# Moving three products of the last Strassen block into the accumulation banks of the plain products, and splitting the last one

## The chip, the cores and the metric

The kernel runs on one core of a Trainium2 chip. The metric is the device time of one execution in microseconds. A profiled execution has a span of its own (first to last instruction), which is a little shorter than its device time.

## The reference

One layer of a decoder trunk on x (512 tokens x 1024). The change touches only the second half of the layer: the squared-ReLU MLP, its addition to the residual stream, and the last LayerNorm.

```python
m = mixer(x, w_in[i], ...)                       # three attention branches, gates, output projection
x = layer_norm(DEEPNORM_ALPHA * x + m, ln1_g[i], ln1_b[i])
hid = jax.nn.relu(x @ w_up[i])                   # 512 x 4096
c = jnp.square(hid) @ w_down[i]                  # 512 x 1024
ple = jax.nn.sigmoid(x @ w_ple_gate[i]) * (p[i] @ w_ple[i])
x = layer_norm(DEEPNORM_ALPHA * x + c + ple, ln2_g[i], ln2_b[i])

def layer_norm(x, g, b):
    mu = x.mean(-1, keepdims=True)
    var = jnp.square(x - mu).mean(-1, keepdims=True)
    return (x - mu) * lax.rsqrt(var + LN_EPS) * g + b
```

## The kernel before

**Numbers as pairs.** Each fp32 matrix is held as a high and a low part in the type fp32r (`h`, `l` or `lo`), and each product of two matrices is three matmuls: high by high, high by low, low by high. A matmul has 128 x 128 weights and up to 512 moving columns, and its result fills a PSUM bank of 128 x 512.

**The list of items.** All large products stand in one list, `items`. An item has its matmuls (`mm`), an evacuation (`ev`) that takes the result out of its bank, the weight chunks that it needs (`need`) and those that it sets free (`c`). The loop at L1157 goes through them in order: an item's evacuation is written down before the matmuls of the next. Banks come from `mm_bank` (two, in turn) or `at_bank` (six). Inside each engine the framework's scheduler then decides the order of the instructions, by its own estimates of when their inputs are there; the engine executes that order strictly.

**Weights.** A chunk of weights is loaded by SP's DMA queue into one of four `raw` buffers, cast to its high part by ScalarE (L209) and its low part taken by VectorE (L210). The pairs lie in rings `wh` and `wl` of seven slots each (`RING`); a slot is taken from those that are free, and a cast waits until one is. `pump` allows a chunk's split as soon as fewer than seven chunks before it are unreleased by the list.

**The MLP.** The 32 column tiles of the hidden layer are made by `up(f)`, 24 matmuls of 512 columns each. The down projection consumes four hidden tiles in a block: seven blocks (`nb = 7`) go by a Strassen scheme, with seven half-size products instead of eight, and the last four tiles by ordinary products, `plain`. A Strassen product `down(b, p, r, ...)` with `p` from 1 to 7 and `r` the upper or lower half of its rows has six matmuls. Products 1, 6 and 7 stay in six `at` banks over all blocks and are combined after the last (L643 to L655). Products 2, 3, 4 and 5 get a bank for each block, and their evacuation adds the result (L638) to one of the eight tiles `acc[tt, half]`: the residual stream in row blocks `tt` = 0 to 3 of 128 tokens and two halves of 512 columns. Products 2, 3 and 4 go to (r, 0), (r, 1) and (r + 2, 0).

`plain` goes through the pairs (tt, half) in the order (0,0), (0,1), (1,0), ... (3,1). Each is a group of 12 matmuls (L668 to L670) in a bank from `mm_bank`; L674 adds the bank to `acc[tt, half]`. For half 0 the first and third of the four plain weight chunks are used in turn, for half 1 the second and fourth. When both halves of a row block are there, its LayerNorm and the two DMAs to the output follow. "Rows 2" below means the row block tt = 2.

**Two LayerNorms.** Rows 0 to 2 use `layer_norm_act`: two passes of ScalarE for the row sums (L425), the mean (L427), two passes of ScalarE for the squares (L429), two small operations (L431, L432), a power on GpSimd (L433), and two scalings of each half on VectorE (L435, L437). Rows 3 use `layer_norm`: `bn_stats` over each half (L408), its aggregate (L410), L412, the power on GpSimd (L413), and scalings L415 and L417.

Of the kernel before, what the change touches and what calls it, by code (L numbers as in the profile page):

```python
# [12 lines left out]
AF = mybir.ActivationFunctionType  # L13
OP = mybir.AluOpType
# [3 lines left out]
P = 128  # L18
FF = 4096
ALPHA = 2.0 ** 0.25  # L20
EPS = 1e-5
# [34 lines left out]
def trunk(tc, a, out):  # L56
    nc = tc.nc
    es = ExitStack()
    with es:
# [14 lines left out]
        def slot(name, dt=F32):  # L74
            return big.tile([P, 512], dt, name=nm(name), tag="s", bufs=NSLOT)

        def small(name, n):
            return one.tile([P, n], F32, name=nm(name), tag=f"sm{n}", bufs=12 if n < 8 else 8)
# [64 lines left out]
        loads, sums, chunks, placed = [], [], [], []  # L143
# [21 lines left out]
        def chunk(src, w):  # L165
            return chunk_of(load(src, w))
# [58 lines left out]
        def item(cs, mm, ev, need=None, bank=None):  # L225
            items.append({"c": cs, "mm": mm, "ev": ev, "need": need, "bank": bank})
# [166 lines left out]
        acc = {}  # L393
        lnc = {}
# [22 lines left out]
                nc.vector.scalar_tensor_tensor(ts[h], ts[h], r, lnc[b][h], op0=OP.mult, op1=OP.add)  # L417
                fin(h, ts[h])

        def layer_norm_act(ts, g, b, fin):  # L420

            sm, sq = small("lsm", 2), small("lsq", 2)
            junk = slot("junk")
            for h in range(2):
                nc.scalar.activation(junk, ts[h], AF.Copy, accum_out=sm[:, h:h + 1])  # L425
            nmu = small("lnm", 1)
            nc.vector.tensor_scalar(nmu, sm[:, 0:1], sm[:, 1:2], -1.0 / D, op0=OP.add, op1=OP.mult)  # L427
            for h in range(2):
                nc.scalar.activation(junk, ts[h], AF.Square, bias=nmu, accum_out=sq[:, h:h + 1])  # L429
            r = small("lr", 1)  # L430
            nc.vector.tensor_scalar(r, sq[:, 0:1], sq[:, 1:2], 1.0 / D, op0=OP.add, op1=OP.mult)  # L431
            nc.vector.tensor_scalar(r, r, EPS, None, op0=OP.add)  # L432
            nc.gpsimd.tensor_tensor(r, r, mhalf, OP.pow)  # L433
            for h in range(2):
                nc.vector.scalar_tensor_tensor(ts[h], ts[h], nmu, lnc[g][h], op0=OP.add, op1=OP.mult)  # L435
            for h in range(2):
                nc.vector.scalar_tensor_tensor(ts[h], ts[h], r, lnc[b][h], op0=OP.mult, op1=OP.add)  # L437
                fin(h, ts[h])
# [109 lines left out]
        left = {}  # L548
# [6 lines left out]
        def mlp_items():  # L555
            nb = 7
# [57 lines left out]
            def down(b, p, r, c, free=()):  # L614

                last = b == nb - 1
                stays = p in (1, 6, 7)

                def bank():
                    if b == 0:  # L620
                        keep[p, r] = at_bank()
                    return keep[p, r]

                def mm(ps):
                    q = slice(r * P, r * P + P)
                    for i in range(2):
                        h, lo = left[2 * b + i, p]
                        s = slice(i * 512, i * 512 + 512)
                        go = i == 0 and (b == 0 or not stays)
                        end = i == 1 and (last or not stays)  # L630
                        nc.tensor.matmul(ps, h[:, q], c["h"][:, s], start=go, stop=False, skip_group_check=True)  # L631
                        nc.tensor.matmul(ps, h[:, q], c["l"][:, s], start=False, stop=False, skip_group_check=True)  # L632
                        nc.tensor.matmul(ps, lo[:, q], c["h"][:, s], start=False, stop=end, skip_group_check=True)  # L633

                def ev(ps):
                    if not stays:
                        t = acc[{2: (r, 0), 3: (r, 1), 4: (r + 2, 0), 5: (r + 2, 1)}[p]]
                        nc.vector.tensor_add(t, t, ps)  # L638
                    if (p, r) in ((6, 0), (7, 0)):
                        left_rest()  # L640
                    if not last:
                        return
                    if p == 1:  # L643
                        p1s[r] = slot("p1s")
                        nc.scalar.copy(p1s[r], ps)
                        nc.vector.tensor_add(acc[r, 0], acc[r, 0], ps)
                    elif p == 6:
                        v3[r] = slot("v3")
                        nc.vector.tensor_sub(v3[r], ps, p1s[r])
                        nc.vector.tensor_add(acc[r, 1], acc[r, 1], v3[r])  # L650
                        nc.vector.tensor_add(acc[r, 1], acc[r, 1], acc[r + 2, 1])
                    elif p == 7:
                        nc.vector.tensor_add(v3[r], v3[r], ps)
                        nc.vector.tensor_sub(acc[r + 2, 0], acc[r + 2, 0], v3[r])
                        nc.vector.tensor_add(acc[r + 2, 1], acc[r + 2, 1], v3[r])  # L655
                item(list(free), mm, ev, need=[c], bank=bank if stays else None)

            def plain(cs):

                for tt in range(4):  # L660
                    for half in range(2):
                        def mm(ps, tt=tt, half=half):
                            q = slice(tt * P, tt * P + P)
                            for i in range(4):
                                h, lo = left[4 * nb + i]
                                c = cs[i % 2, half]
                                s = slice((i // 2) * 512, (i // 2) * 512 + 512)
                                nc.tensor.matmul(ps, h[:, q], c["h"][:, s], start=i == 0, stop=False)  # L668
                                nc.tensor.matmul(ps, h[:, q], c["l"][:, s], start=False, stop=False)
                                nc.tensor.matmul(ps, lo[:, q], c["h"][:, s], start=False, stop=i == 3)  # L670

                        def ev(ps, tt=tt, half=half):
                            t = acc[tt, half]
                            nc.vector.tensor_add(t, t, ps)  # L674
                            if half:
                                def fin(h, y):
                                    (nc.sync if h else nc.scalar).dma_start(
                                        out[0, tt * P:tt * P + P, 512 * h:512 * h + 512], y)
                                norm = layer_norm if tt == 3 else layer_norm_act
                                norm([acc[tt, 0], acc[tt, 1]], "ln2_g", "ln2_b", fin)  # L680
                        item(list(cs.values()) if (tt, half) == (3, 1) else [], mm, ev, need=list(cs.values()))

            for f in range(4):
                up(f)
            for b in range(nb):
                wd = a["wd"][b]
                ld = lambda i: load(wd[i].rearrange("p k n -> p (k n)"), 1024)
                up(4 * b + 4)
                s11 = ld(0)
                s12 = ld(1)  # L690
                t1 = total(s11, s12)
                c5 = chunk_of(t1)
                c1 = chunk_of(s11)
                down(b, 5, 0, c5)
                down(b, 1, 0, c1)
                down(b, 5, 1, c5, [c5])
                cu = up(4 * b + 5, False)
                s22 = ld(3)
                t2 = total(t1, s22)
                t3 = total(s12, s22)  # L700
                c3 = chunk_of(s22)
                c6 = chunk_of(t2)
                down(b, 3, 0, c3)
                down(b, 1, 1, c1, [c1, cu])
                down(b, 6, 0, c6)
                down(b, 3, 1, c3, [c3])
                cu = up(4 * b + 6, False)
                s21 = ld(2)
                c2 = chunk_of(s21)
                down(b, 2, 0, c2)  # L710
                down(b, 6, 1, c6, [c6, cu])
                down(b, 2, 1, c2, [c2])
                up(4 * b + 7)
                c7 = chunk_of(t3)
                c4 = chunk_of(total(t2, s21))
                down(b, 4, 0, c4)
                down(b, 7, 0, c7)
                down(b, 7, 1, c7, [c7])
                down(b, 4, 1, c4, [c4])
            wd = a["wd"][nb]  # L720
            plain({(i // 2, i % 2): chunk(wd[i].rearrange("p k n -> p (k n)"), 1024) for i in range(4)})

        wout_at = len(items)
        ple_items()
# [17 lines left out]
        mhalf = one.tile([P, 1], F32, name="mhalf")  # L742
# [79 lines left out]
        for i in range(2):  # L822
            nc.vector.scalar_tensor_tensor(lamt[:, 2 * i, :], lamt[:, 2 * i, :], 1.0, lamt[:, 2 * i + 1, :],
                                           op0=OP.mult, op1=OP.mult, accum_out=lp[:, i:i + 1])
# [332 lines left out]
        for n, it in enumerate(items):  # L1157
# [3 lines left out]
            need = it["need"] or it["c"]  # L1161
# [18 lines left out]
            ps = it["bank"]() if it["bank"] else mm_bank()  # L1180
# [106 lines left out]
```

## Time and profile before

| what | value |
|---|---|
| median of 3 runs | 1104.25 us (1103.94 to 1104.48) |
| profiled execution: device time | 1104.82 us |
| profiled execution: span | 1103.1 us |
| mean granted TensorE clock | 0.996 |
| TensorE matmul busy | 1084.1 us (98%) |
| VectorE busy | 682.4 us (62%) |
| ScalarE busy | 481.7 us (44%) |
| GpSimd busy | 38.8 us (4%) |

How to read the rows: `PE` is TensorE's matmuls, `PEld` its weight loads, `DVE` VectorE, `ACT` ScalarE, `POOL` GpSimd, `SP` SyncE; a name with a q (`ACTq`) is that engine's queue issuing something. A row of a timeline gives start (us), duration (us), engine, line, operation, tiles written and read, shape, and in brackets the idle time of the engine before it with what ended that. A row of a group ends in its busy time, the mean in ns of one and the idle time before them. A row of the windows gives the stretch, its length, the busy time of each engine, the granted clock, the DMA engines' busy share, and GB/s.

### The profile page before, as it was taken

How to read it: one execution, taken by the hardware profiler on the slowest of the kernel's cores; microseconds unless marked ns; L12 is line 12 of the kernel's file. 1: busy time of each engine (PE TensorE's matmuls, PEld its weight loads, DVE VectorE, ACT ScalarE, POOL GpSimd, SP SyncE). 2: the span in 40 equal slices, each digit the busy share in tenths (PEclk: the TensorE clock that was granted, in tenths of full speed). 3: DMA queues.
4: the chain of work that ended last, by engine and by line, in shares of the span. 5: the costliest groups of instructions: out<-in, count | busy, mean ns of one | idle time of the engine just before them, and what ended most of it. 6: DMA issues, size and time to landing. Idle time of an engine off the chain costs nothing.

```text
span 1103.1 us, 13166 instructions
## 1 busy us (share of the span) xinstructions
PE 1084.1 (98%) x5032; PEld 898.6 (81%) x5032; DVE 682.4 (62%) x1216; ACT 481.7 (44%) x803; POOL 38.8 (4%) x74
## 2 busy tenths in 40 slices
PE   8999999999999999899999999999999999999996
PEld 5888788999888887778888888888888888888884
DVE  6868466564253758654444354875676686686676
ACT  7656444343232545453233232333554454454433
POOL 1000200000000000000000020110000000000000
PEclk9999999999999999999999999999999999999999
DMA  8222422131222103113322344243222322322302
GB/s 271 103 96 84 135 77 77 39 102 50 98 77 87 59 27 105 58 52 102 105 86 96 105 143 163 77 153 113 97 96 77 134 96 80 131 96 95 115 1 76
DMA packets 31327, 105.71 MB, mean 96 GB/s; under 512 B 3962, under 2 KB 4106, under 8 KB 31264
## 3 DMA queue, kind: packets, MB, share of 16 engines
q1 hardware_dynamic: 28080, 96.48, 25.6%
q0 software_dynamic: 2608, 7.35, 2.2%
q10 hardware_dynamic: 576, 1.05, 0.3%
q8 instruction: 39, 0.64, 0.2%
q14 instruction: 24, 0.20, 0.1%
HBM read 102.74 MB, written 2.12 MB: 95 GB/s over the span
## 4 chain that ended last, share of the span: by engine, by line
PE 90%; DVE 5%; ACT 2%; issue 1%; DMA 1%; POOL 1%; SPq 0%; DVEq 0%; ACTq 0%; POOLq 0%
PE mm L88 17%; PE mm L89 17%; PE mm L87 17%; PE mm L299 3%; PE mm L301 3%; PE mm L300 3%; PE mm L632 2%; PE mm L631 2%; PE mm L633 2%; PE at L632 2%; PE at L631 2%; PE at L633 2%; PE mm L462 1%; PE mm L460 1%; PE mm L527 1%; PE mm L528 1%
## 5 line engine op out<-in xcount | busy, mean ns | idle before, releaser
L209 ACT CAST wh<-raw 128x1024 fp32r<-128x1024 f32 (+2 forms) x176 | 180.4, 1027 | 295.9 <-PE mm L88 237.9
L210 DVE TENSOR_TENSOR wl<-raw,wh 128x1024 fp32r<-128x1024 f32 (+2 forms) x176 | 209.0, 1192 | 120.8 <-ACT wh L209 119.2
L87 PE MATMUL mm<-xhT,wh 128*128 128x512 f32 x512 | 203.1, 397 | 0.9 <-DVE da_qb L108 0.7
L88 PE MATMUL mm<-xlT,wh 128*128 128x512 f32 x512 | 200.9, 392 | 1.6 <-DVE xlT L210 1.6
L89 PE MATMUL mm<-xhT,wl 128*128 128x512 f32 x512 | 201.2, 393 | 0.5 <-DVE wl L210 0.5
L88 PEld LDWEIGHTS mm<-xlT,wh 128*128 128x128 f32 x512 | 96.5, 188 | 22.4 <-DVE xlT L210 3.5
L87 PEld LDWEIGHTS mm<-xhT,wh 128*128 128x128 f32 x512 | 96.6, 189 | 20.6 <-DVE da_qb L108 1.1
L89 PEld LDWEIGHTS mm<-xhT,wl 128*128 128x128 f32 x512 | 96.3, 188 | 20.5 <-DVE wl L210 1.0
L88 PE MATMUL mm<-x1lT,wh 128*128 128x512 f32 x256 | 99.6, 389 | 0.0
L89 PE MATMUL mm<-x1hT,wl 128*128 128x512 f32 x256 | 99.6, 389 | 0.0
L87 PE MATMUL mm<-x1hT,wh 128*128 128x512 f32 x256 | 99.6, 389 | 0.0
L299 PE MATMUL mm<-wh,xhT 128*128 128x512 f32 x160 | 65.5, 410 | 0.0
L300 PE MATMUL mm<-wl,xhT 128*128 128x512 f32 x160 | 63.2, 395 | 0.0
L301 PE MATMUL mm<-wh,xlT 128*128 128x512 f32 x160 | 63.2, 395 | 0.0
L87 PEld LDWEIGHTS mm<-x1hT,wh 128*128 128x128 f32 x256 | 48.1, 188 | 10.0
L89 PEld LDWEIGHTS mm<-x1hT,wl 128*128 128x128 f32 x256 | 48.1, 188 | 10.0
L88 PEld LDWEIGHTS mm<-x1lT,wh 128*128 128x128 f32 x256 | 48.1, 188 | 9.9
L209 ACT CAST wh<-wsum 128x1024 fp32r<-128x1024 f32 x28 | 29.5, 1053 | 52.7 <-PE mm L88 49.3
L210 DVE TENSOR_TENSOR wl<-wsum,wh 128x1024 fp32r<-128x1024 f32 x28 | 34.3, 1224 | 23.7 <-ACT wh L209 23.1
L638 DVE TENSOR_TENSOR xn<-xn,mm 128x512 f32<-128x512 f32 x56 | 38.2, 682 | 9.9 <-PE mm L633 9.8
L632 PE MATMUL mm<-wl,hh 128*128 128x512 f32 x112 | 43.6, 389 | 0.0
L631 PE MATMUL mm<-wh,hh 128*128 128x512 f32 x112 | 43.6, 389 | 0.0
(302 smaller groups left out, 1948.9 us busy)
## 6 DMA issues: line engine op xcount, KB each, us to landing
raw<-in_wt_dram SPq DMA_DIRECT2D x63, 512.0 KB, 3.3
raw<-in_wu_dram SPq DMA_DIRECT2D x32, 512.0 KB, 3.3
raw<-in_wd_dram SPq DMA_DIRECT2D x32, 512.0 KB, 3.2
raw<-in_wv_dram SPq DMA_DIRECT2D x20, 512.0 KB, 3.3
raw<-in_wb_dram SPq DMA_DIRECT2D x8, 512.0 KB, 3.3
raw<-in_wo_dram SPq DMA_DIRECT2D x8, 512.0 KB, 3.6
raw<-in_wg_dram SPq DMA_DIRECT2D x8, 512.0 KB, 5.0
rawx<-in_xT_dram SPq DMA_DIRECT2D x8, 256.0 KB, 7.2
```

What stands on the lines that cost most here:

```text
L87: nc.tensor.matmul(ps, wh, xh, start=start, stop=False, skip_group_check=True)
L88: nc.tensor.matmul(ps, wh, xl, start=False, stop=False, skip_group_check=True)
L89: nc.tensor.matmul(ps, wl, xh, start=False, stop=stop, skip_group_check=True)
L209: nc.scalar.copy(h, raw)
L210: nc.vector.tensor_sub(lo, raw, h.bitcast(F32))
L299: nc.tensor.matmul(ps, x1, c["h"][:, s], start=k == 0, stop=False)
L300: nc.tensor.matmul(ps, x1, c["l"][:, s], start=False, stop=False)
L301: nc.tensor.matmul(ps, x2, c["h"][:, s], start=False, stop=k == 7)
L631: nc.tensor.matmul(ps, h[:, q], c["h"][:, s], start=go, stop=False, skip_group_check=True)
L632: nc.tensor.matmul(ps, h[:, q], c["l"][:, s], start=False, stop=False, skip_group_check=True)
L633: nc.tensor.matmul(ps, lo[:, q], c["h"][:, s], start=False, stop=end, skip_group_check=True)
L638: nc.vector.tensor_add(t, t, ps)
```

## The change

In the last Strassen block (b = 6) the products 2, 3 and 4, six items of six matmuls, are no longer items. Their matmuls open the bank of the plain group that adds to the same tile, so six of the eight groups have more matmuls: (0,0), (1,0) take product 2, (0,1), (1,1) product 3, and (2,0), (3,0) product 4. The weight chunks `c2`, `c3` and `c4` and the hidden tiles of these products are held until the lower half has read them: until (1,0), (1,1) and (3,0). Number and size of the chunks' loads and rings stay.

For rows 0 to 2 the addition becomes a `scalar_tensor_tensor` with an accumulator output, which writes the row sum of its half; the two ScalarE passes of `layer_norm_act` for the sums are gone.

For rows 3 the banks come from `at_bank`; the group (3,1) is cut into two parts of 256 columns with a bank each. Every part's addition is followed by `bn_stats` over it, and a new `last_norm` aggregates three sets of statistics, scales the two halves by L415's operation, and then makes L417's operation in three parts (512, 256 and 256 columns), each with its own output DMA on the SP, ScalarE and SP queues.

```diff
-        def layer_norm_act(ts, g, b, fin):
+        def layer_norm_act(ts, sm, g, b, fin):
 
-            sm, sq = small("lsm", 2), small("lsq", 2)
+            sq = small("lsq", 2)
             junk = slot("junk")
-            for h in range(2):
-                nc.scalar.activation(junk, ts[h], AF.Copy, accum_out=sm[:, h:h + 1])
...
-            def plain(cs):
+            def plain(cs, c2, c3, c4):
+                sums = {}
+                s6 = slot("bn6e")[:, :18].rearrange("p (a b) -> p a b", b=6)
+                ends = [(0, slice(0, 512)), (1, slice(0, 256)), (1, slice(256, 512))]
+
+                def part(tt, half, cc):
+                    n = cc.stop - cc.start
+                    r = tt % 2
+                    p, cp = {(0, 0): (2, c2), (0, 1): (3, c3), (1, 0): (4, c4)}.get((tt // 2, half), (0, None))
+
+                    def mm(ps):
+                        q = slice(r * P, r * P + P)
+                        for i in range(2 if p else 0):
+                            h, lo = left[2 * nb - 2 + i, p]
+                            s = slice(i * 512, i * 512 + 512)
+                            nc.tensor.matmul(ps, h[:, q], cp["h"][:, s], start=i == 0, stop=False)
+                            nc.tensor.matmul(ps, h[:, q], cp["l"][:, s], start=False, stop=False)
+                            nc.tensor.matmul(ps, lo[:, q], cp["h"][:, s], start=False, stop=False)
+                        q = slice(tt * P, tt * P + P)
+                        for i in range(4):
+                            h, lo = left[4 * nb + i]
+                            c = cs[i % 2, half]
+                            s = slice((i // 2) * 512 + cc.start, (i // 2) * 512 + cc.stop)
+                            nc.tensor.matmul(ps[:, :n], h[:, q], c["h"][:, s], start=i == 0 and not p, stop=False)
+                            nc.tensor.matmul(ps[:, :n], h[:, q], c["l"][:, s], start=False, stop=False)
+                            nc.tensor.matmul(ps[:, :n], lo[:, q], c["h"][:, s], start=False, stop=i == 3)
+
+                    def ev(ps):
+                        t = acc[tt, half]
+                        if tt < 3:
+                            if not half:
+                                sums[tt] = small("lsm", 2)
+                            nc.vector.scalar_tensor_tensor(t, t, 1.0, ps, op0=OP.mult, op1=OP.add,
+                                                           accum_out=sums[tt][:, half:half + 1])
                             if half:
...
+                                layer_norm_act([acc[tt, 0], acc[tt, 1]], sums[tt], "ln2_g", "ln2_b", fin)
+                            return
+                        nc.vector.tensor_add(t[:, cc], t[:, cc], ps[:, :n])
+                        nc.vector.bn_stats(s6[:, ends.index((half, cc)), :], t[:, cc])
+                        if (half, cc) == ends[2]:
+                            last_norm()
+                    free = [cp] if p and r else []
+                    if (tt, half, cc) == (3, *ends[2]):
+                        free = list(cs.values())
+                    item(free, mm, ev, need=list(cs.values()) + ([cp] if p else []),
+                         bank=at_bank if tt == 3 else None)
+
+                def last_norm():
+                    ts = [acc[3, 0], acc[3, 1]]
+                    mv = small("mv", 2)
+                    nc.vector.bn_aggr(mv, s6)
+                    r = small("lr", 1)
+                    nc.vector.tensor_scalar(r, mv[:, 1:2], EPS, None, op0=OP.add)
+                    nc.gpsimd.tensor_tensor(r, r, mhalf, OP.pow)
+                    for h in range(2):
+                        nc.vector.scalar_tensor_tensor(ts[h], ts[h], mv[:, 0:1], lnc["ln2_g"][h], op0=OP.subtract,
+                                                       op1=OP.mult)
+                    for i, (h, cc) in enumerate(ends):
+                        nc.vector.scalar_tensor_tensor(ts[h][:, cc], ts[h][:, cc], r, lnc["ln2_b"][h][:, cc],
+                                                       op0=OP.mult, op1=OP.add)
+                        (nc.scalar if i == 1 else nc.sync).dma_start(
+                            out[0, 3 * P:4 * P, 512 * h + cc.start:512 * h + cc.stop], ts[h][:, cc])
+
+                for tt in range(3):
+                    for half in range(2):
+                        part(tt, half, slice(0, 512))
+                for half, cc in ends:
+                    part(3, half, cc)
...
-                down(b, 3, 0, c3)
+                if b < nb - 1:
+                    down(b, 3, 0, c3)
                 down(b, 1, 1, c1, [c1, cu])
                 down(b, 6, 0, c6)
-                down(b, 3, 1, c3, [c3])
+                if b < nb - 1:
+                    down(b, 3, 1, c3, [c3])
...
-            plain({(i // 2, i % 2): chunk(wd[i].rearrange("p k n -> p (k n)"), 1024) for i in range(4)})
+            plain({(i // 2, i % 2): chunk(wd[i].rearrange("p k n -> p (k n)"), 1024) for i in range(4)}, c2, c3, c4)
```

The calls of `down(b, 2, ...)` and `down(b, 4, ...)` get the same condition.

More of the change, by code (lines that the diff above doesn't have):

```diff
@@ L656, in down @@
                 item(list(free), mm, ev, need=[c], bank=bank if stays else None)
-            def plain(cs):
[L660 to L674, printed above, removed]
+            def plain(cs, c2, c3, c4):
[29 more added lines that the diff above has]
+                                                           accum_out=sums[tt][:, half:half + 1])
@@ L678, in fin @@
                                         out[0, tt * P:tt * P + P, 512 * h:512 * h + 512], y)
-                                norm = layer_norm if tt == 3 else layer_norm_act
-                                norm([acc[tt, 0], acc[tt, 1]], "ln2_g", "ln2_b", fin)
-                        item(list(cs.values()) if (tt, half) == (3, 1) else [], mm, ev, need=list(cs.values()))
+                                layer_norm_act([acc[tt, 0], acc[tt, 1]], sums[tt], "ln2_g", "ln2_b", fin)
[29 more added lines that the diff above has]
+                    part(3, half, cc)
             for f in range(4):
@@ L709, in mlp_items @@
                 c2 = chunk_of(s21)
-                down(b, 2, 0, c2)
+                if b < nb - 1:
+                    down(b, 2, 0, c2)
                 down(b, 6, 1, c6, [c6, cu])
-                down(b, 2, 1, c2, [c2])
+                if b < nb - 1:
+                    down(b, 2, 1, c2, [c2])
                 up(4 * b + 7)
@@ L715, in mlp_items @@
                 c4 = chunk_of(total(t2, s21))
-                down(b, 4, 0, c4)
+                if b < nb - 1:
+                    down(b, 4, 0, c4)
                 down(b, 7, 0, c7)
                 down(b, 7, 1, c7, [c7])
-                down(b, 4, 1, c4, [c4])
+                if b < nb - 1:
+                    down(b, 4, 1, c4, [c4])
             wd = a["wd"][nb]
-            plain({(i // 2, i % 2): chunk(wd[i].rearrange("p k n -> p (k n)"), 1024) for i in range(4)})
+            plain({(i // 2, i % 2): chunk(wd[i].rearrange("p k n -> p (k n)"), 1024) for i in range(4)}, c2, c3, c4)
         wout_at = len(items)
```

## The prediction

> **What bounds the kernel now.** I read the page's engine line first, then the timeline of each engine over the last 50 us, since every changed line acts there.
>
> ```profile
> PE 1084.1 (98%) x5032; PEld 898.6 (81%) x5032; DVE 682.4 (62%) x1216; ACT 481.7 (44%) x803; POOL 38.8 (4%) x74
> ```
>
> TensorE is busy for 98% of the span, so until its last matmul the kernel is a matmul stream, and only fewer columns or a gap removed would shorten it. The timeline of PE from the first matmul of the plain products on:
>
> ```profile
> 1070.63 0.39 PE L668 MATMUL mm<-wh,hh 128*128 128x512 f32 x1
> ...
> 1089.44 0.39 PE L670 MATMUL mm<-wh,hl 128*128 128x512 f32 x1
> 1090.40 0.50 PE L668 MATMUL mm<-wh,hh 128*128 128x512 f32 x1 [0.56 <-DVE xn L674]
> ...
> 1093.07 0.39 PE L670 MATMUL mm<-wh,hl 128*128 128x512 f32 x1
> ```
>
> From 1070.63 to 1089.44 lie 83 steps, so one step is 0.2267 us (the 0.39 is one matmul's length; they overlap). Eighty-four matmuls run without a gap. Then the last group starts at 1090.40 instead of 1089.67: it waits 0.73 us for L674, an addition that frees its bank. Now the timeline of DVE behind that:
>
> ```profile
> 1089.66 0.68 DVE L674 TENSOR_TENSOR xn<-xn,mm 128x512 f32<-128x512 f32 x1
> 1091.20 0.21 DVE L427 TENSOR_SCALAR lnm<-lsm 128x1 f32<-128x1 f32 x1 [0.85 <-ACT junk L425]
> 1091.33 0.68 DVE L674 TENSOR_TENSOR xn<-xn,mm 128x512 f32<-128x512 f32 x1
> 1092.04 0.70 DVE L408 BATCH_NORM_STATS2 bn<-xn 128x6 f32<-128x512 f32 x1
> 1092.65 0.73 DVE L435 SCALAR_TENSOR_TENSOR xn<-xn,lnm,ln_g 128x512 f32<-128x512 f32 x1
> 1093.30 0.21 DVE L431 TENSOR_SCALAR lr<-lsq 128x1 f32<-128x1 f32 x1
> 1093.42 0.74 DVE L435 SCALAR_TENSOR_TENSOR xn<-xn,lnm,ln_g 128x512 f32<-128x512 f32 x1
> 1094.08 0.15 DVE L432 TENSOR_SCALAR lr<-lr 128x1 f32<-128x1 f32 x1
> 1094.15 0.68 DVE L674 TENSOR_TENSOR xn<-xn,mm 128x512 f32<-128x512 f32 x1
> 1094.96 1.42 DVE L437 SCALAR_TENSOR_TENSOR xn<-xn,lr,ln_b 128x512 f32<-128x512 f32 x2
> 1096.29 0.69 DVE L408 BATCH_NORM_STATS2 bn<-xn 128x6 f32<-128x512 f32 x1
> 1097.01 0.21 DVE L410 BATCH_NORM_AGGREGATE mv<-bn 128x2 f32<-128x12 f32 x1
> 1097.26 0.15 DVE L412 TENSOR_SCALAR lr<-mv 128x1 f32<-128x1 f32 x1
> 1097.33 1.40 DVE L415 SCALAR_TENSOR_TENSOR xn<-xn,mv,ln_g 128x512 f32<-128x512 f32 x2
> 1098.65 1.41 DVE L417 SCALAR_TENSOR_TENSOR xn<-xn,lr,ln_b 128x512 f32<-128x512 f32 x2
> ```
>
> Here lies the bound of the last 10 us. The matmuls end at 1093.46, but the norm of rows 2 (L427 to L437) is still on DVE and shares it with the norm of rows 3: the last L674 starts 0.7 us late, and its L408 only at 1096.29, behind the two L437 of rows 2. Rows 2 are late because their own addition (the first line) came at 1089.66, though its products were complete near 1087.15 (1089.44 is the twelfth matmul behind them: 1089.67 - 12 x 0.2267 + 0.2). So DVE's queue is the bound, from 1087 to 1100.06. In it the next instruction starts 0.08 us before the one ahead ends (L408 is at 1092.04 with 0.70, its successor at 1092.65), so 0.68 us occupy it for 0.60 and the two L437 for 1.33.
>
> **The change part by part.** *Six down products move.* They are 36 matmuls of 512 columns, before and after; 36 x 0.2267 = 8.16 us leave block 6 and come back inside the plain groups, where a product's two halves open the bank instead of its own item. PE's time: nothing. Six L638 additions disappear from DVE (operation and size of L674, 0.60 us each), in a stretch that PE covers: nothing. What matters is where the 8.16 us are put: the plain stage starts at 1070.63 - 8.16 = 1062.47, and all groups but (2,1) and the last have 18 matmuls (4.08 us) instead of 12 (2.72 us). So groups end, and additions can start 0.2 us behind (a group's last matmul ends 0.16 us after its successor's start, and DVE picks up within 0.04), at: (1,1) 1078.99, (2,0) 1083.07, (2,1) 1085.79, (3,0) 1089.87. Rows 2 are thereby complete 1.36 us earlier than they could be before, and, since a norm takes 6.6 us at most (1089.66 to 1096.29 above) and rows 1 now come 6.8 us earlier, at 1078.99, nothing of rows 1 is still in DVE's queue: their addition starts 3.9 us earlier than the trace's 1089.66.
>
> *The row sums.* The sums move from six ACT passes (L425) into the additions:
>
> ```profile
> 1091.44 0.73 ACT L429 ACTIVATE junk<-xn,lnm 128x512 f32<-128x512 f32 x1 [0.28 <-DVE lnm L427]
> 1092.29 0.72 ACT L429 ACTIVATE junk<-xn,lnm 128x512 f32<-128x512 f32 x1
> ```
> ```profile
> L823 DVE DVE_READ_ACCUMULATOR lamt<-lamt x2: 88/88/88, 15.1 to 15.3; 128x1 f32 x2
> ```
>
> The L427 wait of 0.85 us goes; in its place comes the read of the accumulator, 0.09 us for each of six additions, 0.54 in all, which lies in DVE's idle time except the last ones (0.1). Rows 2 then go: addition 1085.79 to 1086.5, L427 to 1086.75, two L429 of 0.85 to 1088.45, L431, L435, L432 to 1089.4, GpSimd's power, and L437. GpSimd's rows:
>
> ```profile
> 1094.38 0.55 POOL L433 TENSOR_TENSOR lr<-lr,mhalf 128x1 f32<-128x1 f32 x1 [6.08 <-DVE lr L432]
> 1097.55 0.92 POOL L413 TENSOR_TENSOR lr<-lr,mhalf 128x1 f32<-128x1 f32 x1 [2.63 <-DVE lr L412]
> ```
>
> With 0.15 of issue and 0.55 of work L437 can start at 1090.1, against 1094.96.
>
> *The last product in two parts of 256 columns.* The nearest rows are half-wide matmuls, each with a weight load of its own as in every product here (its 188 ns in the second view), and half-wide DVE operations back to back:
>
> ```profile
> 206.24 0.28 PE L898 MATMUL at<-spl,ones_r 128*128 128x256 f32 x1
> 206.36 0.28 PE L898 MATMUL at<-sph,ones_r 128*128 128x256 f32 x1
> ```
> ```profile
> L89 PEld LDWEIGHTS mm<-xhT,wl 128*128 128x128 f32 x512 | 96.3, 188 | 20.5 <-DVE wl L210 1.0
> ```
> ```profile
> 968.94 0.42 DVE L607 TENSOR_TENSOR s<-hid 128x256 f32<-128x256 f32 x1
> 969.28 0.42 DVE L608 TENSOR_TENSOR s<-hid,s 128x256 f32<-128x256 f32 x1
> ```
>
> Twenty-four steps of 0.12 are 2.88 us against 12 x 0.2267 = 2.72: +0.16 on PE. If the loads bound the steps, each would be 0.19, 4.56 us in all or +1.8; I take 0.12, since the rows have the type (fp32r) and the loads of the new matmuls. So the parts can be added from 1091.3 and 1092.75. The three groups of rows 3 get banks of their own, free since block 6: the 0.73 us wait goes.
>
> *The sum at the end.* From 1089.87 on DVE has: addition (3,0) 0.60, its L408 0.61, two L437 1.33, then addition and statistics of each part, 4 x 0.34, with 0.08 for the last one's tail: 3.98 us, so the last statistics end at 1093.85 if DVE never idles, and not before 1092.75 + 0.34 + 0.42 = 1093.5 by PE. If L437 stands ahead of (3,0)'s addition it is 1094.1. In the trace it is 1096.98. Gain: 3.1 us, or 2.9 to 3.5.
>
> Behind the statistics the chain keeps its operations (L410, L412, two L415, hidden power, first L417); L417's second half becomes two parts with a third DMA, two steps of 0.34 to 0.40 instead of 0.66: up to 0.15 more. The outputs leave at the DMA's rate:
>
> ```profile
> 1100.50:1101.00 0.50, 0.00 (x0) 0.00 (x0) 0.00 (x0) 0.00 (x0) 0.00 (x0) 0.50 1.03 381
> ```
> ```profile
> DMA to landing us min/median/max: 2.0/2.1/2.8
> ```
>
> At 381 GB/s the 512 KB take 1.38 us in one piece from the first issue on, and the third part (128 KB, 0.34 us) is issued 0.8 us behind the first, so it joins the piece: no change, between -0.3 (a smaller last transfer) and +0.3 (one more issue in a queue). I take a gain of 3.1 - 0.15 - 0.05 = 2.9 us.
>
> The profiled execution took 1104.82 us with its span of 1103.1, 0.57 over the median of 1104.25; I take the gain off the median: 1104.25 - 2.9 = 1101.35, say 1101.4 us.
>
> The Trainium skill (VectorE: DVE Perf Modes, section The TRN2 errata) speaks against smaller parts: every VectorE instruction pays a fixed time, so tiles of 512 and more are advised. By its formula for fp32 additions, (N+151)/0.96 ns, each halving would cost 0.157 us; three on the path, as an estimate from that page, would be 0.47 and the result 1101.7. The trace agrees on the length of one (0.68 and 0.42 us) but shows the next starting 0.08 us before its end. The same skill (DMA: Bandwidth & Descriptors, section on the two cost components, 2.0 us plus bytes/436e3) would let a last transfer of half the bytes land 0.3 us sooner, an estimate from that page that gives 1101.1; the row above shows data in one piece at the rate's limit, so I count nothing.
>
> **The rivals.** *Another order on DVE.* DVE works in order, and before it had the last L674 ahead of rows 2's L437. Should the two L437 stand behind the last addition again, the last statistics start 1.33 us later than 1093.09, at 1094.4, and end at 1094.85: gain 2.1 less 0.2, 1102.3 us. For it: the trace's order; against: L437 is ready 2.6 us before the last part is.
>
> *A short gap at the seam.* The weights of products 2, 3 and 4 (three of seven ring slots) are held into the plain groups, so the plain weights' splits start later. In the trace:
>
> ```profile
> 1050.43 1.06 ACT L209 CAST wh<-raw 128x1024 fp32r<-128x1024 f32 x1 [1.19 <-PE mm L633]
> ...
> 1059.95 1.06 ACT L209 CAST wh<-raw 128x1024 fp32r<-128x1024 f32 x1 [0.30 <-PE mm L633]
> ```
> ```profile
> 1059.75 1.22 DVE L210 TENSOR_TENSOR wl<-raw,wh 128x1024 fp32r<-128x1024 f32 x1
> ...
> 1068.11 0.69 DVE L653 TENSOR_TENSOR v<-v,at 128x512 f32<-128x512 f32 x1
> ```
>
> These are the first and last of the casts of the four plain weights, done 10 us before use, and each waits for a slot. Afterwards slots come free behind the second last `up`, product 6, the last `up` and product 7, counted back from 1062.47 by their matmuls: 12 of product 7 (2.72 us) put the end of the last `up` at 1059.75, its 24 (5.44) put that of product 6 at 1054.31, whose 6 (1.36) put that of the `up` before at 1052.95. The third's low half is ready at 1059.75 + 1.05 + 1.22 and gaps, 1062.2, and is read by the eleventh plain matmul, at 1062.47 + 10 x 0.2267 = 1064.74; the fourth's at 1065, read by the 29th, at 1068.82. Covered by 2.5 and 3.8 us, unless DVE puts the six L653 to L655 (one shown; 0.60 each, 3.6 us) first: then a gap of 1.1 us and a gain near 1.8, 1102.4.
>
> *Slower: the ring starves PE.* If no slot comes free before product 7 ends at 1062.47 (held weights, and the rest read until then), all four casts start there: 62.67 + 3 x 1.05 puts the third cast at 1065.8, its low half, third in DVE's queue, at 1067.3, or 1070.9 with the 3.6 us ahead. Read at 1064.74, that is a gap of 2.6 to 6.2 us. From 2.9 it eats the whole gain; at 6.2 the time is 1107.6. Against: three of the slots belong to weights whose last reader is done by 1059.75.
>
> *The end does not move*, because the sums or the three-part norm wait for something unseen and eat the 3 us: 1104.2.
>
> **How the numbers follow.** Forecast 0.59; order on DVE 0.13; short gap 0.10; end unmoved 0.06; ring starves PE 0.12. A measurement of this kernel tells 0.2% (2.2 us) from no change, so faster means below 1102.05. The forecast's whole span (gains of 2.4 to 3.5) lies there, and 0.03 of the order rival, which sits at the edge: faster 0.62. The rest of that rival (0.10), the short gap, the unmoved end and the ring with a gap below 5.1 us (0.03) are the same: 0.29. The ring with a longer gap is slower: 0.09. The range begins with the forecast's best case (3.5 by PE's bound and 0.25 at the DMA: 1100.5) and ends behind the order rival and the gap rival with twice its gap (1102.4 + 1.1 = 1103.5, to 1103.6); the unmoved end and the ring, 0.18, are left out.
>
> **What would show it.** Right: no gap on PE between the last `up` and the end but for issue; last matmul near 1092.7; rows 2's addition near 1085.8; no L425; the last statistics ending at 1093.8 to 1094.2, span near 1100.2. Wrong: a PE idle of over 0.5 us ahead of the first matmul that reads the third or fourth plain weight; half-wide matmuls 0.19 apart; rows 2's last two scalings behind the last addition.

## The result and the profile after

The changed kernel takes 1101.8 us (median of 20 runs, 1100.86 to 1105.42) against 1104.45 (20 runs, 1103.04 to 1106.86): a ratio of 0.9978, 95% interval 0.9972 to 0.9985, or 2.4 us (1.7 to 3.1) faster. Forecast were 1101.4 us and a gain of 2.9. The gain is at the bound of 0.2% that the prediction set for what a measurement tells; the trace shows it more sharply. The engine line of the page:

```profile
PE 1084.2 (99%) x5044; PEld 899.5 (82%) x5044; DVE 679.0 (62%) x1219; ACT 477.0 (43%) x791; POOL 38.9 (4%) x74
```

TensorE's work is unchanged (1084.1 before), with twelve more matmuls from the cut; the span went from 1103.1 to 1100.5. The timeline of PE, from the first matmul of the plain groups:

```profile
1062.56 0.39 PE L674 MATMUL mm<-wh,hh 128*128 128x512 f32 x1
...
1089.76 0.28 PE L682 MATMUL at<-wh,hh 128*128 128x256 f32 x1
...
1092.51 0.28 PE L684 MATMUL at<-wh,hl 128*128 128x256 f32 x1
```

No row carries an idle time: 120 matmuls of 512 columns take 1089.76 - 1062.56 = 27.2 us, 0.2267 each, and the 24 of 256 columns go at (1092.51 - 1089.76) / 23 = 0.12. Before, the last group waited 0.73 us. The timeline of DVE, from the addition (2,1) on:

```profile
1085.88 0.69 DVE L691 SCALAR_TENSOR_TENSOR xn<-xn,mm 128x512 f32<-128x512 f32 x1 [0.44 <-PE mm L684]
...
1087.71 0.75 DVE L433 SCALAR_TENSOR_TENSOR xn<-xn,lnm,ln_g 128x512 f32<-128x512 f32 x1 [0.88 <-ACT junk L427]
...
1090.22 1.42 DVE L435 SCALAR_TENSOR_TENSOR xn<-xn,lr,ln_b 128x512 f32<-128x512 f32 x2 [0.73 <-POOL lr L431]
1091.56 1.01 DVE L699 TENSOR_TENSOR xn<-xn,at 128x512 f32<-128x512 f32 x2
1092.48 1.01 DVE L700 BATCH_NORM_STATS2 bn6e<-xn 128x6 f32<-128x512 f32 x2
1093.41 0.40 DVE L699 TENSOR_TENSOR xn<-xn,at 128x256 f32<-128x256 f32 x1
1093.85 0.43 DVE L700 BATCH_NORM_STATS2 bn6e<-xn 128x6 f32<-128x256 f32 x1
1094.31 0.24 DVE L712 BATCH_NORM_AGGREGATE mv<-bn6e 128x2 f32<-128x18 f32 x1
...
1095.97 1.54 DVE L720 SCALAR_TENSOR_TENSOR xn<-xn,lr,ln_b 128x512 f32<-128x512 f32 x3
```

The addition of rows 2 now waits for PE (0.44 us), where it had come 2.5 us late; the scalings of rows 2 (L435) start at 1090.22 instead of 1094.96; the last statistics end at 1094.28 instead of 1096.98. Of that lead of 2.70 us, 2.55 is left at the end of L720 (1097.51 against 1100.06), and 2.6 in the span.

**A measure that spans don't blur.** The code ahead of block 6 is the same in all kernels here, but in ten profiled executions it took up to 3.4 us more or less. Much of that is the granted clock: the windows show stretches at half clock, none in E3, E4, E7 and E8 below, one near 460 us in the kernel before, the changed one, E5 and E6, and two in E1 and E2. In E1 the clock is 0.69 and 0.74 over 113 to 116 and 116 to 119 us, and 0.72 and 0.71 over 461 to 464 and 464 to 467: each stretch takes 1.7 us. From 1060 to 1093 us the clock is 1.00 in all ten. So kernels are compared by their *tail*: the span's end minus the moment at which PE would be done if no gap came after the first plain matmul (its start plus 0.2267 us for each 512 columns left; below, "PE's undisturbed end"). Before: 1070.63 + 96 x 0.2267 = 1092.39, tail 10.71. After: 1062.56 + 132 x 0.2267 = 1092.48, tail 8.02, thus 2.69 shorter. The page gives spans to a tenth of a microsecond, and each tail comes from one profiled execution, so a difference under about 0.1 us says nothing.

### The profile page after: what moved, and what is told of

It reads as the page before. It is cut to its first block, busy times and chain, and to the rows that moved or that the text cites. A ratio compares the mean times of both kernels' runs of the same rounds, so it can differ in the third digit from the quotient of the medians.

```text
span 1100.5 us, 13179 instructions
## 1 busy us (share of the span) xinstructions
PE 1084.2 (99%) x5044; PEld 899.5 (82%) x5044; DVE 679.0 (62%) x1219; ACT 477.0 (43%) x791; POOL 38.9 (4%) x74
## 4 chain that ended last, share of the span: by engine, by line
PE 92%; DVE 3%; ACT 2%; issue 1%; DMA 1%; SPq 1%; POOL 0%; DVEq 0%; ACTq 0%; POOLq 0%
PE mm L88 17%; PE mm L89 17%; PE mm L87 17%; PE mm L299 3%; PE mm L301 3%; PE mm L300 3%; PE mm L630 2%; PE mm L629 2%; PE mm L631 2%; PE at L630 2%; PE at L629 2%; PE at L631 2%; PE mm L526 1%; PE mm L458 1%; PE mm L525 1%; PE mm L459 1%
## 5 line engine op out<-in xcount | busy, mean ns | idle before, releaser
L301 PEld LDWEIGHTS mm<-wh,xlT 128*128 128x128 f32 x160 | 38.0, 238 | 3.8
L300 PEld LDWEIGHTS mm<-wl,xhT 128*128 128x128 f32 x160 | 38.2, 239 | 3.3
L299 PEld LDWEIGHTS mm<-wh,xhT 128*128 128x128 f32 x160 | 38.0, 238 | 3.4
```

What stands on the lines that cost most here:

```text
L299: nc.tensor.matmul(ps, x1, c["h"][:, s], start=k == 0, stop=False)
L300: nc.tensor.matmul(ps, x1, c["l"][:, s], start=False, stop=False)
L301: nc.tensor.matmul(ps, x2, c["h"][:, s], start=False, stop=k == 7)
```

## Experiments

Theory A is the prediction's: VectorE's queue is in order, rows 2's norm stood in it ahead of rows 3's statistics, and whatever brings rows 2 earlier shortens the tail until PE's end bounds it. Rival B: the removed ScalarE passes are the gain. Rival C: the own banks and the smaller last part are. E1 to E4 do parts of the change alone. Each ratio is to runs of the kernel before in the same comparison. "Statistics" is the end of the last statistics behind PE's undisturbed end.

| kernel | first plain matmul | PE's undisturbed end | statistics | tail | ratio to before (95%) |
|---|---|---|---|---|---|
| before | 1070.63 | 1092.39 | 4.59 | 10.71 | 1 |
| changed | 1062.56 | 1092.48 | 1.80 | 8.02 | 0.9978 (0.9972 to 0.9985) |
| E1 move only | 1064.62 | 1094.54 | 1.89 | 7.96 | 0.9982 (0.9974 to 0.9991) |
| E2 sums only | 1072.23 | 1093.99 | 2.91 | 9.01 | 0.9985 (0.9976 to 0.9993) |
| E3 banks and parts only | 1070.23 | 1091.99 | 5.10 | 11.31 | 1.0008 (0.9999 to 1.0016) |
| E4 sums, banks and parts | 1069.54 | 1091.30 | 2.91 | 9.10 | 0.9986 (0.9978 to 0.9995) |
| E5 changed, rows 2 by bn_stats | 1062.15 | 1092.07 | 1.23 | 7.43 | 0.9967 (0.9954 to 0.9980) |
| E6 move, rows 2 by bn_stats | 1062.70 | 1092.62 | 1.61 | 7.78 | 0.9971 (0.9960 to 0.9983) |
| E7 changed, scalings earlier in line | 1061.19 | 1091.11 | 1.53 | 7.79 | one run |
| E8 changed, scalings behind the last addition | 1061.49 | 1091.41 | 2.44 | 8.69 | one run |

### E1: the move alone

Against the changed kernel, sums, banks, parts and the new norm are undone; the six products stay in the plain groups.

```diff
-                            nc.vector.scalar_tensor_tensor(t, t, 1.0, ps, op0=OP.mult, op1=OP.add,
-                                                           accum_out=sums[tt][:, half:half + 1])
+                            nc.vector.tensor_add(t, t, ps)
...
+                                norm = layer_norm if tt == 3 else layer_norm_act
+                                norm([acc[tt, 0], acc[tt, 1]], "ln2_g", "ln2_b", fin)
...
-                    item(free, mm, ev, need=list(cs.values()) + ([cp] if p else []),
-                         bank=at_bank if tt == 3 else None)
+                        item(free, mm, ev, need=list(cs.values()) + ([cp] if p else []))
```

> Only the move: the six products of block 6 go into the plain groups; row sums stay ScalarE passes, rows 3 keep the two mm banks, the whole last product and the old norm. Theory A (VectorE's in-order queue: the gain is that rows 2's norm gets out of the way of rows 3, by whatever means it comes earlier): addition (2,1) starts within 0.1 us of its products, no gap on PE, last statistics end 1.9 us behind PE's undisturbed end (before: 4.6), so 2.7 us faster than before, the whole gain of the change. Rival B (the removed ScalarE passes make the gain): under 1 us faster. Rival C (own banks and smaller last part make it): no faster.

The tail is 7.96 us, 2.75 shorter than before: the move alone gives the whole gain in the trace, and in time it is 0.18% faster (0.09 to 0.26). The timeline of DVE in E1:

```profile
1087.94 0.69 DVE L684 TENSOR_TENSOR xn<-xn,mm 128x512 f32<-128x512 f32 x1 [0.23 <-PE mm L680]
...
1093.10 1.42 DVE L437 SCALAR_TENSOR_TENSOR xn<-xn,lr,ln_b 128x512 f32<-128x512 f32 x2
1094.43 0.69 DVE L408 BATCH_NORM_STATS2 bn<-xn 128x6 f32<-128x512 f32 x1
1095.03 0.67 DVE L684 TENSOR_TENSOR xn<-xn,mm 128x512 f32<-128x512 f32 x1
1095.74 0.69 DVE L408 BATCH_NORM_STATS2 bn<-xn 128x6 f32<-128x512 f32 x1
```

The addition (2,1) waits for PE, so rows 2 are on time, and PE has no gap although the groups share the two old banks. B and C fall: the gain needs neither the sums nor the banks and parts.

### E2: the sums alone

Against the kernel before, for rows 0 to 2 only:

```diff
-            for h in range(2):
-                nc.scalar.activation(junk, ts[h], AF.Copy, accum_out=sm[:, h:h + 1])
...
-                            nc.vector.tensor_add(t, t, ps)
...
+                                nc.vector.scalar_tensor_tensor(t, t, 1.0, ps, op0=OP.mult, op1=OP.add,
+                                                               accum_out=sums[tt][:, half:half + 1])
```

> Only the row sums: additions of rows 0 to 2 write the sums, ScalarE's two passes for each are gone; all else as before. Theory A: each of the three norms is 0.85 us shorter and the backlog shrinks by that each time: addition (2,1) near 2.1 us earlier than before, at 0.45 us behind its products, PE's 0.73 us gap gone, last statistics end 1.7 us earlier: 1.7 us faster. Rival B: 2.4 to 2.7 us faster, all of the gain. Rival C: no faster.

The tail is 1.70 us shorter, as A has it, and not the 2.4 to 2.7 of B. The last two groups are 24 steps, 5.44 us, and an addition can start 0.2 us behind its group, so the products of rows 2 are there 5.24 us ahead of PE's undisturbed end: at 1093.99 - 5.24 = 1088.75 in E2 (before: 1092.39 - 5.24 = 1087.15). Their addition comes at 1089.24: 0.5 us late instead of 2.5. PE's timeline has no gap here either. DVE's lines:

```profile
1089.24 0.68 DVE L677 SCALAR_TENSOR_TENSOR xn<-xn,mm 128x512 f32<-128x512 f32 x1
1089.84 0.08 DVE L677 DVE_READ_ACCUMULATOR xn<-xn,mm 128x1 f32 x1
...
1092.76 0.68 DVE L680 TENSOR_TENSOR xn<-xn,mm 128x512 f32<-128x512 f32 x1
1093.57 1.41 DVE L435 SCALAR_TENSOR_TENSOR xn<-xn,lr,ln_b 128x512 f32<-128x512 f32 x2
1094.90 0.69 DVE L408 BATCH_NORM_STATS2 bn<-xn 128x6 f32<-128x512 f32 x1
1095.51 0.67 DVE L680 TENSOR_TENSOR xn<-xn,mm 128x512 f32<-128x512 f32 x1
1096.21 0.69 DVE L408 BATCH_NORM_STATS2 bn<-xn 128x6 f32<-128x512 f32 x1
```

So the parts don't add: 1.70 and 2.75 alone, 2.69 in the changed kernel. Both draw on the same backlog.

### E3: own banks and parts alone

Against the changed kernel, move and sums are undone: the six items of block 6 are back, `layer_norm_act` is the old one.

```diff
+                    p, cp = 0, None
...
-                            nc.vector.scalar_tensor_tensor(t, t, 1.0, ps, op0=OP.mult, op1=OP.add,
-                                                           accum_out=sums[tt][:, half:half + 1])
+                            nc.vector.tensor_add(t, t, ps)
```

> Only the end: own banks for rows 3, last product in two parts of 256 columns, norm in three parts; no move, row sums by ScalarE. Theory A: PE's gap goes, but VectorE's queue is as late as before and holds two more instructions on the way: last statistics end 0.4 us later than before, and the time is 0.3 to 0.6 us slower. Rival C: 1 us or more faster, since the gap of 0.73 us and the smaller last part save it. Rival B: no change.

The tail grows by 0.60 us (time: between 0.01% faster and 0.16% slower). The timeline of DVE in E3 says why:

```profile
1093.74 0.41 DVE L699 TENSOR_TENSOR xn<-xn,at 128x256 f32<-128x256 f32 x1
1094.55 1.41 DVE L437 SCALAR_TENSOR_TENSOR xn<-xn,lr,ln_b 128x512 f32<-128x512 f32 x2 [0.40 <-POOL lr L433]
1095.88 0.42 DVE L700 BATCH_NORM_STATS2 bn6e<-xn 128x6 f32<-128x256 f32 x1
1096.22 0.41 DVE L699 TENSOR_TENSOR xn<-xn,at 128x256 f32<-128x256 f32 x1
1096.66 0.43 DVE L700 BATCH_NORM_STATS2 bn6e<-xn 128x6 f32<-128x256 f32 x1
```

PE's last matmul started at 1092.02, without a gap ahead of it, but what it brought is added only at 1096.22, behind the two L437 of rows 2. These start 2.56 us behind PE's undisturbed end, against 2.57 before (1094.96): with PE's gap of 0.73 us or without it, so the gap cost nothing. Behind them stood one statistic, and now there are three instructions: more work behind a full queue costs its own length. C falls.

### E4: the changed kernel without the move

```diff
+                    p, cp = 0, None
...
-                if b < nb - 1:
-                    down(b, 3, 0, c3)
+                down(b, 3, 0, c3)
```

The other five items come back in the same way.

> The changed kernel without the move: sums with the additions, own banks, parts; the six products stay items of block 6. Theory A: as with the sums alone, last statistics 1.6 us earlier than before, 1.5 us faster: 1.2 us short of the changed kernel. Rival B: the whole gain, 2.4 to 2.7 us. Rival C: between, more than with the sums alone by 0.7.

The tail is 9.10, 1.61 shorter than before (0.14% faster in time, 0.05 to 0.22): within 0.1 us the gain of the sums alone. The move is worth another 1.08 on top.

### E5: rows 2 take their statistics on VectorE

```diff
+                        if tt == 2:
+                            nc.vector.tensor_add(t, t, ps)
...
+                            nc.vector.bn_stats(st2[0][:, half, :], t)
+                            if half:
+                                rows2_norm(st2[0])
+                            return
                         if tt < 3:
```

`rows2_norm` has the operations of `layer_norm` behind its statistics, and rows 2's two output DMAs.

> The changed kernel, but rows 2 take their statistics on VectorE (as rows 3 do) in place of ScalarE's squares. Theory A (VectorE's queue still bounds the last 4 us of the changed kernel): two more statistics fall into VectorE's idle time, rows 2's last scaling ends near 90.35 on the changed kernel's clock instead of 91.6, and the last statistics end 0.7 us earlier, bounded by PE: end of the span 7.3 to 7.4 us behind PE's undisturbed end instead of 8.0; 0.6 us faster than the changed kernel, 3.3 faster than before. Rival (the changed kernel's tail is already bound by PE and the chain of rows 3): no change, 8.0.

The tail is 7.43 us, 0.59 shorter than the changed kernel's. The rival falls: VectorE's queue still bounded the changed kernel, with the norm of rows 2 in it. It was not full there. Its rows in the section on the result wait 0.88 us for ScalarE's squares and 0.73 us for GpSimd's power, while the addition (3,0) stands behind. Now PE is the bound, at the last addition:

```profile
1088.73 1.41 DVE L730 SCALAR_TENSOR_TENSOR xn<-xn,lr,ln_b 128x512 f32<-128x512 f32 x2
1090.06 0.68 DVE L707 TENSOR_TENSOR xn<-xn,at 128x512 f32<-128x512 f32 x1
...
1092.42 0.42 DVE L707 TENSOR_TENSOR xn<-xn,at 128x256 f32<-128x256 f32 x1 [0.17 <-PE at L684]
1092.87 0.43 DVE L708 BATCH_NORM_STATS2 bn6e<-xn 128x6 f32<-128x256 f32 x1
```

In time it is 1101.24 against 1104.66 of before in the same comparison: 0.33% faster (0.20 to 0.46). Its interval overlaps that of the changed kernel, so the 0.6 us between the two rest on the trace alone.

### E6: only the move, and rows 2's statistics on VectorE

Against E1:

```diff
-                                norm = layer_norm if tt == 3 else layer_norm_act
+                                norm = layer_norm if tt >= 2 else layer_norm_act
```

> The move and rows 2's statistics on VectorE, nothing else: no sums with the additions, no own banks, the last product whole. Theory A: rows 2 are out of the way, so the end is PE's end, one whole addition and one whole statistic (1.5 us) and the old norm: span 7.6 us behind PE's undisturbed end, 3.1 us faster than before and 0.4 faster than the changed kernel with less of the change in it. Rival (the smaller last part is needed to come under the changed kernel): 8.0 or more.

The tail is 7.78 us against an expected 7.6, 0.24 under the changed kernel: with neither sums, banks nor parts. Its last addition waited 0.71 us for PE:

```profile
1092.82 0.69 DVE L684 TENSOR_TENSOR xn<-xn,mm 128x512 f32<-128x512 f32 x1 [0.71 <-PE mm L680]
1093.54 0.69 DVE L408 BATCH_NORM_STATS2 bn<-xn 128x6 f32<-128x512 f32 x1
```

E5's tail is 0.35 us shorter, 0.3 if one allows for the rounded spans. In both kernels PE has no gap and the last addition waits for it, so what differs behind it is the smaller last part, with the norm in three parts: that is what the parts bring once PE is the bound.

### E7 and E8: where rows 2's last scalings stand in the queue

Rows 2's last two scalings are taken out of `layer_norm_act` and queued behind another VectorE instruction, `first`: in E7 the statistics of (3,0), in E8 the last addition.

```diff
+                with tc.issue_after(getattr(first, "ins", first)):
+                    for h in range(2):
+                        nc.vector.scalar_tensor_tensor(ts[h], ts[h], r, lnc[b][h], op0=OP.mult, op1=OP.add)
```

> The changed kernel with rows 2's last two scalings held behind the first half's statistics of rows 3. Theory A: VectorE's 0.4 us of idleness ahead of the scalings is filled, last statistics end 0.1 to 0.3 us earlier: span 7.7 to 7.9 us behind PE's undisturbed end. Rival (order is of no weight): 8.0.

> The changed kernel with rows 2's last two scalings held behind the last addition, the order that the prediction had as a rival. Theory A: 1.33 us of scalings then stand between the last addition and its statistics; last statistics end 0.65 us later than in the changed kernel: span 8.6 to 8.7 us behind PE's undisturbed end. Rival (order is of no weight): 8.0.

The tails are 7.79 and 8.69 us, against 8.02 with the scheduler's own order. The scalings and what stands behind them, first in E7, then in E8:

```profile
1089.92 1.40 DVE L437 SCALAR_TENSOR_TENSOR xn<-xn,lr,ln_b 128x512 f32<-128x512 f32 x2
1091.24 0.74 DVE L710 TENSOR_TENSOR xn<-xn,at 128x256 f32<-128x256 f32 x2
```

```profile
1091.76 0.42 DVE L710 TENSOR_TENSOR xn<-xn,at 128x256 f32<-128x256 f32 x1 [0.55 <-PE at L694]
1092.10 1.41 DVE L437 SCALAR_TENSOR_TENSOR xn<-xn,lr,ln_b 128x512 f32<-128x512 f32 x2
1093.43 0.42 DVE L713 BATCH_NORM_STATS2 bn6e<-xn 128x6 f32<-128x256 f32 x1
```

In E8 the last addition, at 1091.76, had waited 0.55 us for PE, and its statistics started 1.67 us later, at 1093.43, with both scalings in between. The order alone is worth 0.9 us in the trace; in time each of the two has one run, which can't tell.

## Why the prediction was right, and where not

**The bound and the move.** That DVE's queue bounded the last 10 us, and PE did not, is shown by E3 (PE's gap gone, the end later) and by E1 (rows 2 on time, the whole gain). The plain groups start at 1062.56 (forecast 1062.47), and rows 2's addition at 1085.88 (1085.8). That such moments agree to 0.1 us is in part luck: both traces hold one stretch at half clock, and in E1, with two, the plain groups start at 1064.62.

**The sum at the end.** The last statistics end at 1094.28; the forecast had 1093.85, and 1094.1 with the scalings (L435, in the kernel before L437) ahead of (3,0)'s addition. The 0.43 us are three mis-sizings. The stage starts 0.09 later. The other order came: L435 waits 0.73 us for GpSimd, and the addition (3,0), whose products are there at 1089.96, stands behind it (0.25). And I took a step of 0.34 for each half-wide instruction, but where one reads what the last one wrote, it is 0.44 (1093.41, 1093.85, and its end at 1094.28): 4.06 us from 1090.22 on, where I had 3.98 (0.1). Behind that, I took off 0.2 for the third output and it was 0.1, so the trace has 2.6 us in place of 2.9.

**What gave the gain.** Here a step failed, though the sum didn't. The prediction counted the lost 0.85 us wait of L427 and the own banks as sources beside the move. E1 shows that the move needs neither: rows 2 are then early enough even with the ScalarE passes, and PE's gap goes by itself when the addition (2,1) is on time. Sums, banks and parts take nothing off the changed kernel's tail (8.02 with them, 7.96 without), although without the move they are worth 1.61 (E4).

**The seam.** The rivals of a short gap and of a starved PE did not come. The third and fourth plain weights, on ACT and on DVE:

```profile
1059.81 1.05 ACT L209 CAST wh<-raw 128x1024 fp32r<-128x1024 f32 x1 [3.13 <-PE mm L88]
...
1062.76 1.06 ACT L209 CAST wh<-raw 128x1024 fp32r<-128x1024 f32 x1
```

```profile
1060.90 1.23 DVE L210 TENSOR_TENSOR wl<-raw,wh 128x1024 fp32r<-128x1024 f32 x1 [0.83 <-ACT wh L209]
...
1064.53 1.22 DVE L210 TENSOR_TENSOR wl<-raw,wh 128x1024 fp32r<-128x1024 f32 x1
```

The third cast came with its slot's release (1059.81, forecast 1059.75), the fourth at 1062.76, and the low halves were ready at 1062.13 and 1065.75 (forecast 1062.2 and 1065), 2.7 and 3.2 us ahead of their readers. The fourth's stood 0.7 us in DVE's queue behind additions that the gap rival named, two instead of six. How much longer slots could be held was not tried.

**The order on DVE.** The rival was real but not taken: in E8 it costs 0.67 us over the scheduler's order. The prediction had its last statistics end at 1094.85, 0.75 us behind the 1094.1 of the order that came.

**Smaller parts.** They cost what the prediction took on PE (0.12 us a step) and for L720 (1.54 against 1.41). The Trainium skill's advice in VectorE: DVE Perf Modes (The TRN2 errata), against pieces under 512, holds while the queue is full (E3, +0.60) and turns once VectorE waits for PE (E5 against E6, about -0.3). The prediction's 1101.7 for it doesn't follow from its own terms: it had counted 0.30 us for the three halvings, and 0.47 in their place makes 1101.35 into 1101.5. The rule of the Trainium skill in DMA: Bandwidth & Descriptors (Two cost components), a fixed part plus bytes, which the page fits to DMAs on GpSimd's path, would by estimate have had the halved output land 0.3 us sooner. Here SP and ScalarE issue the outputs, and the source view of the last three DMAs has no such difference, the same 2.1 for 256 and 128 KB:

```profile
DMA to landing us min/median/max: 2.1/2.1/2.1
```

## What to carry to other kernels

When a strictly ordered engine's queue is the bound at a kernel's end, ask which older work stands in it ahead of the last result, and give that work its inputs earlier; moving matmuls that must be done anyway from before to between the last groups did this at no cost. Fixes that drain the same backlog don't add up, and a gap on the busiest engine is worth nothing while another queue ends later. Cut the last piece smaller only once the queue that takes it up waits for it.

## What was not expected of the hardware

The same code, up to the last Strassen block, placed the first plain matmul of the move's kernels between 1061.19 us (E7, no stretch at half clock) and 1064.62 (E1, two stretches, 3.4 us lost). That is 3.4 us, more than the whole change, so a span alone could have ranked these kernels wrongly. Over all ten kernels the stretches leave up to 1.6 us unexplained, and why one execution has them and another doesn't is not shown. The mean granted clock is a rough guide only, for it also counts the clock behind TensorE's last matmul (0.52 over 1095 to 1098 us in the changed kernel).
